# Down projection of a decoder trunk: three of each eight channel-block pairs by seven products of block sums

## The chip, the cores and the metric

The kernel runs on one core of a Trainium2 chip. The metric is the device time in microseconds (us) of one execution. The engines are named PE (TensorE, matmuls), DVE (VectorE), ACT (ScalarE), POOL (GpSimd) and SP (SyncE, which issues most DMAs); PEld is the weight load of TensorE, which overlaps its matmuls.

## The reference

Two decoder layers on 256 tokens with a model width of 2048, all in float32. Each layer has an attention part (two head groups) and an MLP with 8192 hidden channels:

```python
mixed = jnp.concatenate([o_gla, o_sb], axis=-1)
x = x + jnp.einsum('bse,ed->bsd', mixed, w_o)

hm = rms_norm(x, mlp_norm)
up = jnp.square(jax.nn.relu(jnp.einsum('bsd,df->bsf', hm, w_up)))
return x + jnp.einsum('bsf,fd->bsd', up, w_down)
```

The change concerns the last line: 256 tokens x 8192 channels times a 8192 x 2048 matrix, once in each of two layers, added to the residual.

## The kernel before

Every float32 factor is cut into an exact high and a low part of the type fp32r, and a product is three matmuls: high by high, high by low, low by high. For weights, ACT copies the loaded tile `raw` into the high part `whi` (L325), and DVE subtracts it for the low part `wlo` (L327), in pieces of 128 x 1024 numbers. `whi` and `wlo` have four buffers each and `raw` three, so the splits run ahead of the matmuls by up to four pieces (half-units).

The MLP goes through the 8192 hidden channels in four quarters of 2048. For a quarter, up projection (`mlp_up`) makes 16 blocks of 128 channels, with the channels on partitions: `unit_t` computes 256 columns (L391, L395), `join` adds the high and the low sums (ACT copy L405, DVE add L406), then come relu with the norm's row (L888), square (L892), and the split into high and low activations (L893, L894). Down projection (`mlp_down(q)`) then multiplies the quarter by its 2048 rows of `w_down`, in four units of 512 columns. A unit (`unit`) is 16 channel blocks x 2 token tiles x 3 matmuls of 128 x 512 (L344, L345, L346) into two PSUM banks, the tile `acc`; at its end DVE adds the unit to the residual `xb` (L919, 128 x 1024; at the program's end L910 with a store). PSUM holds two `acc` tiles of two banks each and four single banks `ps`, for the whole program.

The code's order is six groups of up (of four in a quarter, two units each), down of the first quarter, four groups of up, and so on. The framework has a scheduler that orders each engine's queue anew; the order on an engine is therefore not that of the code. Each engine works off its queue in order.

At a layer's end (`residual`) the residual blocks also go through transposes on PE (`norm_operand`, L261), which make the next layer's operand, and through sums of squares.

The functions that the change touches:

Of the kernel before, what the change touches and what calls it, by code (L numbers as in the profile page):

```python
# [39 lines left out]
def trunk_kernel(  # L40
# [19 lines left out]

    cpool = ctx.enter_context(tc.tile_pool(name="const", bufs=1))
# [5 lines left out]
    accp = ctx.enter_context(tc.tile_pool(name="acc", bufs=2, space=PSUM))  # L67
    psp = ctx.enter_context(tc.tile_pool(name="ps", bufs=4, space=PSUM))

    uid = [0]  # L70

    def nm(s):
        uid[0] += 1
        return f"{s}_{uid[0]}"
# [4 lines left out]
    def ps_tile():  # L79
        return psp.tile([P, 512], F32, tag="ps", name=nm("ps"))  # L80

    def acc_tile():
        return accp.tile([P, 2, 512], F32, tag="acc", name=nm("acc"))

    def tmp(tag, shape, dt=F32, bufs=2):
        return tpool.tile(list(shape), dt, tag=tag, name=nm(tag), bufs=bufs)
# [18 lines left out]
    kdz = cpool.tile([P, 3, 512], F32, name="kdz")  # L105

    def build_constants():
        nc.vector.tensor_copy(ident16, ident)

        # strictly causal mask of a diagonal block, keys on partitions: 0 where s < t  # L110
# [5 lines left out]
        # suffix sums: -1 where j >= s (j on partitions)  # L116
# [9 lines left out]
        # 1 where s <= c and both lie in one chunk (s on partitions)  # L126
# [8 lines left out]
        # scan multiplier: 0 at the start of each chunk  # L135
# [4 lines left out]
        # exp(last - cum) * k, tokens on partitions, one chunk's rows kept per entry  # L140
        nc.gpsimd.memset(kdz, 0.0)

# [82 lines left out]
    def inv_rms(ss, n, width):  # L225
        """(ss / width + EPS) ** -0.5, [P, n], with one Newton step."""
# [9 lines left out]
    class Operand:  # L236
        """Activations with channels on partitions: [P, 2 blocks, (high, low), T] tiles."""
# [15 lines left out]
    def norm_operand(op, n, key, l):  # L253
        """Residual block n -> operand blocks 4n.. (scaled by the gain)."""
# [316 lines left out]
    for l in range(DEPTH):  # L571
# [306 lines left out]
        # MLP  # L878
        up = {}

        def mlp_up(i):
            q, g = divmod(i, 4)
            if g == 0:
                up[q] = Operand()
# [83 lines left out]
```

## Time and profile before

| | |
|---|---|
| Time, median of 3 runs (lowest to highest) | 2248.5 us (2248.33 to 2249.91) |
| Profiled execution: span from first to last instruction | 2247.4 us |
| Its own time | some 1.1 us beside the span, if it ran as the median did |
| TensorE clock granted | 1.000 |
| PE busy | 2238.0 us, 11436 matmuls |
| DVE busy | 1315.8 us |
| ACT busy | 1085.9 us |
| Bytes moved, mean rate | 409.04 MB, 182 GB/s |

The runs lie within 1.6 us of each other. The page gives busy time as a share of the span, over all stages; which engine another waits for is in the view of the waits, and what a single stage does is in the windows and the timeline.

### The profile page before, as it was taken

To read this page: it belongs to the slowest core of one execution; us is meant where nothing else is said; L and a number is where in the kernel's file an instruction comes from. 1 tells how busy PE (TensorE), PEld (TensorE's weight loads), DVE (VectorE), ACT (ScalarE), POOL (GpSimd) and SP (SyncE) were. 2 spreads that over 40 slices of the span, in tenths; PEclk is the share of its full clock that TensorE was granted. 3 is DMA by queue.
4 is the path that set the end of the run, shared out by engine and by line. 5 is a ranking of instruction groups with operands and counts; after the bars stand their busy time and mean duration, and the time that the engine had idled before them with its cause. 6 is when DMAs were issued, how large, how long until landed. Compare 5 with 4: busy or idle time off the path is not lost.

```text
span 2247.4 us, 28019 instructions
## 1 busy us (share of the span) xinstructions
PE 2238.0 (100%) x11436; PEld 1883.2 (84%) x11436; DVE 1315.8 (59%) x1508; ACT 1085.9 (48%) x1363; POOL 37.7 (2%) x67
## 2 busy tenths in 40 slices
PE   9999999999999999999999999999999999999999
PEld 7988778888888888888888887888888888888887
DVE  5777565666556556555557765656655554565554
ACT  5555355555345445445445553555543453454442
POOL 0020000000000000000000200000000000000000
PEclk9999999999999999999999999999999999999999
DMA  6555445665565566565546544456665655655554
GB/s 226 190 157 163 150 143 195 187 188 188 200 191 186 190 188 187 190 196 192 180 149 202 169 152 149 164 184 182 191 194 191 187 188 191 192 186 197 189 197 141
DMA packets 283622, 409.04 MB, mean 182 GB/s; under 512 B 6651, under 2 KB 162883, under 8 KB 283493
## 3 DMA queue, kind: packets, MB, share of 16 engines
q1 hardware_dynamic: 283492, 407.24, 56.6%
q8 instruction: 90, 1.47, 0.3%
q14 instruction: 40, 0.32, 0.0%
HBM read 405.12 MB, written 2.10 MB: 181 GB/s over the span
## 4 chain that ended last, share of the span: by engine, by line
PE 98%; DVE 1%; issue 0%; DMA 0%; ACT 0%; POOL 0%; SPq 0%; DVEq 0%; POOLq 0%
PE acc L391 24%; PE acc L344 19%; PE acc L346 19%; PE acc L345 19%; PE acc L395 12%; PE ps L261 1%; PE ps L806 1%; PE ps L818 1%; PE ps L765 0%; PE ps L507 0%; PE ps L453 0%; PE ps L542 0%; PE ps L471 0%; DVE wlo L327 0%; DMA raw<-in_w_in_dram 0%
## 5 line engine op out<-in xcount | busy, mean ns | idle before, releaser
L327 DVE TENSOR_TENSOR wlo<-raw,whi 128x1024 fp32r<-128x1024 f32 (+2 forms) x786 | 944.4, 1204 | 805.2 <-ACT whi L325 804.6
L325 ACT ACTIVATE whi<-raw 128x1024 fp32r<-128x1024 f32 (+2 forms) x786 | 816.4, 1041 | 1036.7 <-PE acc L346 642.8
L391 PE MATMUL acc<-act,whi 128*128 128x512 f32 x2304 | 811.2, 397 | 0.0
L344 PE MATMUL acc<-whi,act 128*128 128x512 f32 (+2 forms) x1984 | 766.6, 386 | 1.4 <-ACT act L269 1.1
L345 PE MATMUL acc<-wlo,act 128*128 128x512 f32 (+2 forms) x1984 | 760.3, 383 | 0.4 <-DVE wlo L327 0.4
L346 PE MATMUL acc<-whi,act 128*128 128x512 f32 (+2 forms) x1984 | 759.9, 383 | 0.0
L395 PE MATMUL acc<-act,wlo 128*128 128x256 f32 x2304 | 644.1, 280 | 0.0
L391 PEld LDWEIGHTS acc<-act,whi 128*128 128x128 f32 x2304 | 432.7, 188 | 104.0
L344 PEld LDWEIGHTS acc<-whi,act 128*128 128x128 f32 x1984 | 372.9, 188 | 76.5 <-issue 4.1
L395 PEld LDWEIGHTS acc<-act,wlo 128*128 128x128 f32 x2304 | 434.4, 189 | 0.4
L346 PEld LDWEIGHTS acc<-whi,act 128*128 128x128 f32 x1984 | 372.7, 188 | 73.8 <-issue 0.7
L345 PEld LDWEIGHTS acc<-wlo,act 128*128 128x128 f32 x1984 | 372.9, 188 | 71.7 <-DVE wlo L327 1.2
L406 DVE TENSOR_TENSOR t<-acc,t 128x512 f32<-128x512 f32 x72 | 49.2, 683 | 0.0
L894 DVE TENSOR_TENSOR act<-t,act 128x512 fp32r<-128x512 f32 x64 | 44.3, 692 | 6.2 <-ACT act L893 6.2
L893 ACT ACTIVATE act<-t 128x512 fp32r<-128x512 f32 x64 | 40.5, 634 | 11.8 <-PE acc L346 10.0
L888 DVE SCALAR_TENSOR_TENSOR t<-t,row 128x512 f32<-128x512 f32 x64 | 44.3, 692 | 2.2
L405 ACT ACTIVATE t<-acc 128x512 f32<-128x512 f32 x72 | 41.6, 578 | 0.0
L892 ACT ACTIVATE t<-t 128x512 f32<-128x512 f32 x64 | 39.4, 615 | 0.0
L919 DVE TENSOR_TENSOR xb<-acc,xb 128x1024 f32<-128x1024 f32 x24 | 29.4, 1224 | 9.6 <-PE acc L346 9.6
L413 DVE TENSOR_REDUCE st<-t 128x4 f32<-128x512 f32 (+1 forms) x36 | 21.6, 622 | 0.5
L301 POOL COPY bc<-st 128x128 f32<-128x128 f32 x8 | 2.6, 320 | 1149.5 <-DVE st L233 1059.9
L412 DVE TENSOR_TENSOR t<-on 128x512 f32<-128x512 f32 x16 | 11.9, 743 | 16.1 <-ACT on L532 16.1
(137 smaller groups left out, 669.4 us busy)
## 6 DMA issues: line engine op xcount, KB each, us to landing
raw<-in_w_up_dram SPq DMA_DIRECT2D x128, 1024.0 KB, 5.8
raw<-in_w_down_dram SPq DMA_DIRECT2D x128, 1024.0 KB, 5.0
raw<-in_w_in_dram SPq DMA_DIRECT2D x84, 1024.0 KB, 5.2
raw<-in_w_o_dram SPq DMA_DIRECT2D x32, 1024.0 KB, 5.1
raw<-in_w_in_dram SPq DMA_DIRECT2D x14, 512.0 KB, 6.7
raw<-in_w_in_dram SPq DMA_DIRECT2D x8, 544.0 KB, 3.9
out_dram<-xb SPq DMA_DIRECT2D x8, 256.0 KB, 2.3
xb<-in_x_dram SPq DMA_DIRECT2D x3, 512.0 KB, 7.9
```

Of the source, the lines that this page charges most:

```text
L325: newest["hi"] = nc.scalar.activation(h, r, AF.Copy).ins
L327: newest["lo"] = nc.vector.tensor_tensor(lo[:, q : q + step, :width], r, f32(h), ALU.subtract).ins
L344: nc.tensor.matmul(o, xh[:, sl], whi[:, j, :width], start=first, stop=False)
L345: nc.tensor.matmul(o, xh[:, sl], wlo[:, j, :width], start=False, stop=False)
L346: st["mm"] = nc.tensor.matmul(o, xl[:, sl], whi[:, j, :width], start=False, stop=last).ins
L391: nc.tensor.matmul(acc[:, f, :], whi[:, j, sl], op.both(k), start=(k == 0), stop=False, skip_group_check=True,)
L395: nc.tensor.matmul(acc[:, f, T:], wlo[:, j, sl], xh, start=False, stop=(k == KT - 1), skip_group_check=True,)
L405: nc.scalar.activation(t, acc[:, :, T:], AF.Copy)
L406: nc.vector.tensor_tensor(t, acc[:, :, :T], t, ALU.add)
L888: nc.vector.scalar_tensor_tensor(t, t, 0.0, nxt["row"].unsqueeze(1).to_broadcast([P, 2, T]), ALU.max, ALU.mult,)
L893: nc.scalar.activation(d[:, :, 0, :], t, AF.Copy)
L894: nc.vector.tensor_tensor(d[:, :, 1, :], t, f32(d[:, :, 0, :]), ALU.subtract)
```

## The change

**Products.** A step of down projection is now one pair of channel blocks (256 channels) by 1024 columns, and a quarter is two halves of eight steps. Tokens, channels and columns are each two blocks, so a step is a 2 x 2 by 2 x 2 block product. For the pairs 1, 4 and 7 (`fast`), it is done by seven block products of sums and differences (Strassen's scheme in Winograd's form), 7 x 3 = 21 matmuls; the other pairs take eight products, 24 matmuls, arranged so that they add into four of the same sums.

**Banks.** The sums of a half stay in seven PSUM banks, `m1` to `m7`, over all eight steps, and are put together in `xb` at the half's end by eleven additions on DVE of 128 x 512 (`plain` and `shared`, L1020) and a copy on ACT (L1104). PSUM is divided anew for that: seven banks and one `ps` during down projection, as before in the rest.

**Weights.** In a fast step DVE forms sums of weight blocks from `raw`: `t13` (L1049, 128 x 1024), a sum in place over the second block (`b12`), and `t4` (L1020, 128 x 512 each). They are split as other weights are (L1002 high, L1005 low). For nine of the ten plain steps of a quarter, the low part of the second half is made otherwise: ACT writes the negative high part (`early`, L997), and a DMA from POOL's queue adds `raw` to it (L998, 512 KB). Raw tiles are 128 x 2 x 1024, three buffers and one more, `raw2`, for each fourth step; a step's load is issued three steps ahead.

**Activations.** After the square of an up unit, `up_forms` makes differences of its 128 x 128 blocks on DVE (L942 to L949): four operations for a fast pair, one for another; ACT and DVE split them too (L933, L934).

**Order.** All four groups of up of a quarter, then its down projection.

The core of the diff:

```diff
+        def up_forms(op, i, t):
+            a11, a21, a12, a22 = (t[:, k, r * P : (r + 1) * P] for k in range(2) for r in range(2))
+            e = tmp("t2", [P, 3, P], bufs=4)
+            if fast(i):
+                d = op.x[i] = tmp("sx", [P, 3, 2, P], F32R, bufs=3)
+                nc.vector.tensor_tensor(e[:, 2, :], a21, a11, ALU.subtract)
+                nc.vector.tensor_tensor(a21, a21, a22, ALU.subtract)
+                nc.vector.tensor_tensor(e[:, 0, :], a11, a21, ALU.subtract)
+                nc.vector.tensor_tensor(e[:, 1, :], a12, e[:, 0, :], ALU.subtract)
+            else:
+                d = op.x[i] = tmp("cx", [P, 2, 2, P], F32R, bufs=5)
+                e = e[:, :2, :]
+                nc.vector.tensor_tensor(e, t[:, :, :P], t[:, :, P:], ALU.subtract)
+            split(op.pair(i), t)
+            split(d, e)
+
+        def fast(i):
+            return i % 3 == 1
...
         def mlp_down(q):
-            for n in range(4):
-                ud = unit(up[q], w_down[l], q * KT * P, n * 512, 512, split=(end and n == 3))
...
+            def early(x):
+                if x in low2 or x >= len(steps) or x == 0 or fast(steps[x][1]):
+                    return
+                r = raws[x][:, :, 512:]
+                lo = low2[x] = act_tile(F32R, (P, 2, 512))
+                nc.scalar.activation(lo, r, AF.Copy, scale=-1.0)
+                nc.gpsimd.dma_start(f32(lo), r, accum_op=ALU.add)
...
+                if fast(j):
+                    t13 = tmp("ts", [P, 2, 512], bufs=2)
+                    t4 = tmp("t4", [P, 512], bufs=1)
+                    b12 = r[:, 0, 512:]
+                    ends = r.rearrange("p k (c n) -> p (k c) n", c=2)[:, ::3, :]
+                    nc.vector.tensor_tensor(
+                        t13, ends, b12.unsqueeze(1).to_broadcast([P, 2, 512]), ALU.add
+                    )
+                    w = parts(r[:, 1, :].rearrange("p (c n) -> p c n", c=2))
+                    mm(2, blk(1, 0), w, 0, final)
+                    mm(3, ext(1), w, 1, final)
+                    add(b12, t13[:, 0, :], r[:, 1, 512:])
+                    add(t4, b12, r[:, 1, :512])
+                    w = parts(t4.unsqueeze(1), 1)
+                    mm(4, blk(1, 1), w, 0, final)
+                    tick()
+                    w = parts(t13)
+                    mm(5, blk(0, 1), w, 0, final)
+                    mm(7, ext(2), w, 1, final_fast)
+                    w = parts(r[:, 0, :].rearrange("p (c n) -> p c n", c=2))
+                    mm(1, blk(0, 0), w, 0, final_fast)
+                    mm(6, ext(0), w, 1, final_fast)
+                    tick()
+                else:
+                    w = parts(r[:, :, :512])
+                    for k in range(2):
+                        mm(2, blk(k, 0), w, k, final and k == 1)
+                        mm(4, blk(k, 1), w, k, final and k == 1)
+                    tick()
+                    w = parts(r[:, :, 512:], lo=low2.get(x))
+                    for k in range(2):
+                        mm(5, blk(k, 1), w, k, final and k == 1)
+                    for k in range(2):
+                        mm(3, ext(k), w, k, final and k == 1)
+                    tick()
...
-        for i in range(6):
-            mlp_up(i)
-        for q in range(3):
+        for q in range(4):
+            if q:
+                att_psum()
+            for g in range(4):
+                mlp_up(q, g)
+            down_psum()
             mlp_down(q)
-            for i in range(6 + 4 * q, min(10 + 4 * q, 16)):
-                mlp_up(i)
-        mlp_down(3)
```

**Two places in the queues.** The first is ACT's queue where up projection gives way to down projection in layer 0's first quarter; the later quarters have the same rows. Before: `raw_819` and the raws after it are weights of later units, `acc_800` is the last up unit and `t2_811` its result on chip.

```order
L325 ACTIVATE whi_822_4770<-raw_819_4752 128x1024
L405 ACTIVATE t2_811_4709<-acc_800_4624 128x512
L325 ACTIVATE whi_825_4788<-raw_824_4786 128x1024
L892 ACTIVATE t2_811_4709<-t2_811_4709 128x512
L325 ACTIVATE whi_827_4804<-raw_824_4786 128x1024
L325 ACTIVATE whi_830_4822<-raw_829_4820 128x1024
```

After: `raw_792` holds the weights of step 1, the first fast one, `t4_803` and `ts_802` (t13) are sums of them; `raw_793` and `raw2_794` are the weights of steps 2 and 3; `t2_778` is the last up unit's result, `t2_779` its differences.

```order
L1002 ACTIVATE whi_804_4467<-raw_792_4418 128x1024
L1002 ACTIVATE whi_806_4479<-t4_803_4465 128x512
L437 ACTIVATE t2_778_4385<-acc_767_4300 128x512
L929 ACTIVATE t2_778_4385<-t2_778_4385 128x512
L1002 ACTIVATE whi_808_4486<-ts_802_4464 128x1024
L933 ACTIVATE act_781_4396<-t2_778_4385 128x2x256
L933 ACTIVATE sx_780_4391<-t2_779_4390 128x3x128
L997 ACTIVATE act_795_4424<-raw_793_4420 128x1024
L997 ACTIVATE act_801_4461<-raw2_794_4422 128x1024
L1002 ACTIVATE whi_810_4496<-raw_792_4418 128x1024
```

The last up unit's copy, square and split stood between high parts for later units. Now they stand, with two more 128 x 1024 copies (L997) and the split of the differences, ahead of the high part `whi_810` that step 1's last six matmuls read.

The second is DVE's queue where the down projection of layer 0's first quarter gives way to up projection (later quarters alike). Before, with the last drain of the quarter in the second row:

```order
L327 TENSOR_TENSOR wlo_905_5315<-raw_903_5312,whi_904_5314 128x1024
L919 TENSOR_TENSOR xb3_99<-acc_876_5131,xb3_99 128x1024
L327 TENSOR_TENSOR wlo_907_5335<-raw_903_5312,whi_906_5334 128x1024
L327 TENSOR_TENSOR wlo_913_5366<-raw_911_5363,whi_912_5365 128x1024
```

After, where `wlo_912` and `wlo_914` are low parts for the last fast step, and `wlo_921` and `wlo_923` those of up projection's first weights, `raw_919`:

```order
L1005 TENSOR_TENSOR wlo_912_5031<-ts_905_5007,whi_911_5029 128x1024
L1020 TENSOR_TENSOR xb2_100<-m2__854_4744,xb2_100 128x512
L1005 TENSOR_TENSOR wlo_914_5041<-raw2_887_4900,whi_913_5039 128x1024
L1020 TENSOR_TENSOR xb2_100<-m4__855_4745,xb2_100 128x512
L1020 TENSOR_TENSOR xb3_101<-m5__857_4747,xb3_101 128x512 x2
L1020 TENSOR_TENSOR xb3_101<-m3__856_4746,xb3_101 128x512
L1020 TENSOR_TENSOR xb2_100<-m1__858_4748,xb2_100 128x512
L359 TENSOR_TENSOR wlo_921_5074<-raw_919_5071,whi_920_5073 128x1024
L1020 TENSOR_TENSOR t2_915_5054<-m6__859_4749,t2_915_5054 128x512
L359 TENSOR_TENSOR wlo_923_5094<-raw_919_5071,whi_922_5093 128x1024
```

One drain of 128 x 1024 stood between low parts made well ahead. Now six drains of 128 x 512 stand between the last fast step's low parts and the first of up projection.

More of the change, by code (lines that the diff above doesn't have):

```diff
@@ L860, in residual @@
         def residual(op, n, key, ll, ssq, acc, done):
-            nc.vector.tensor_tensor(xb[n], acc, xb[n], ALU.add)
+            if acc is not None:
+                nc.vector.tensor_tensor(xb[n], acc, xb[n], ALU.add)
             after(1, lambda: norm_operand(op, n, key, ll))
@@ L902, in mlp_down @@
         def mlp_down(q):
[L903 to L912 removed]
+            op = up[q]
+            end = q == 3 and l + 1 == DEPTH
@@ new lines, in mlp_down, with mm, add @@
+            banks, begun = {}, set()
+            def mm(m, a, w, c, last):
+                (ah, al), (wh, wl) = a, w
+                o = banks[m]
+                nc.tensor.matmul(o, ah, wh[:, c], start=m not in begun, stop=False)
+                begun.add(m)
+                nc.tensor.matmul(o, ah, wl[:, c], start=False, stop=False)
+                nc.tensor.matmul(o, al, wh[:, c], start=False, stop=last)
+            def add(dst, a, b, sub=False):
+                nc.vector.tensor_tensor(dst, a, b, ALU.subtract if sub else ALU.add)
```

159 lines of the change are left out of this document (129 added, 30 removed).

## The prediction

> **What bounds the kernel now.** I read the page first: span, busy time of each engine, and the chain that ended last.
>
> ```profile
> span 2247.4 us, 28019 instructions
> PE 2238.0 (100%) x11436; PEld 1883.2 (84%) x11436; DVE 1315.8 (59%) x1508; ACT 1085.9 (48%) x1363; POOL 37.7 (2%) x67
> PE 98%; DVE 1%; issue 0%; DMA 0%; ACT 0%; POOL 0%; SPq 0%; DVEq 0%; POOLq 0%
> ```
>
> TensorE sets the end nearly alone: 98% of the chain is matmul following matmul. Next the waits by pair (total us, count, longest us).
>
> ```profile
> DVE wlo L327 <- ACT whi L325: 804.6, 641, 4.4
> ACT whi L325 <- PE acc L346: 642.8, 415, 3.9
> PE acc L344 <- ACT act L269: 1.1, 1, 1.1
> ```
>
> The splits wait for TensorE (ScalarE's high part for a buffer that matmuls free, VectorE's low part for the high one); TensorE's own longest such wait on ScalarE adds up to 1.1 us in the whole program. Then two units of a down projection by the window view (after the window: sum, then PE, PEld, DVE, ACT, POOL, granted clock, DMA share, GB/s), and a stretch of up projection.
>
> ```profile
> 574.00:595.75 21.75, 21.75 (x97) 18.02 (x96) 10.93 (x10) 8.48 (x9) 0.00 (x0) 1.00 0.56 193
> 595.75:617.51 21.76, 21.76 (x97) 18.02 (x96) 10.94 (x10) 8.49 (x9) 0.00 (x0) 1.00 0.59 194
> 541.00:552.20 11.20, 11.20 (x66) 9.81 (x66) 6.84 (x7) 5.97 (x8) 0.00 (x0) 1.00 0.57 194
> ```
>
> A unit is 96 matmuls in 21.76 us, so 0.2267 us each at clock 1.00, while VectorE works half of the time, ScalarE 39%, the DMA engines 0.56 to 0.59. So every matmul less is worth 0.2267 us, as long as three engines that have been half idle keep up with a pattern that asks for more of them.
>
> **What the change removes.** A quarter of a layer's down projection had 4 x 96 = 384 matmuls. Now each of its two halves (1024 columns) runs eight steps, one for each pair of channel blocks: five plain steps of 24 matmuls and three seven-product ("fast") steps of 21, so 183 instead of 192. Eight quarters x 18 = 144 matmuls; 144 x 0.2267 = **-32.6 us**. The matmuls keep their shape (128x512). (The Trainium skill, page "TensorE: Matmul & The Clock Gate", section "Back-to-back issue gap", states a sustained 131 ns for N=512; by that the gain would be an estimated 18.9 us. The trace's spacing is 227 ns, and it decides.)
>
> **What it adds.** Durations, by form (count | busy, mean ns):
>
> ```profile
> L327 DVE TENSOR_TENSOR wlo<-raw,whi 128x1024 fp32r<-128x1024 f32 x750 | 919.3, 1228 | 785.2 <-ACT whi L325 784.6
> L327 DVE TENSOR_TENSOR wlo<-raw,whi 128x512 fp32r<-128x512 f32 x20 | 13.6, 686 | 9.9 <-ACT whi L325 9.9
> L325 ACT ACTIVATE whi<-raw 128x1024 fp32r<-128x1024 f32 x750 | 793.6, 1060 | 1003.4 <-PE acc L346 615.7 <-PE acc L391 385.1 <-ACT t L278 1.8
> L406 DVE TENSOR_TENSOR t<-acc,t 128x512 f32<-128x512 f32 x72 | 49.2, 683 | 0.0
> L888 DVE SCALAR_TENSOR_TENSOR t<-t,row 128x512 f32<-128x512 f32 x64 | 44.3, 692 | 2.2
> L833 DVE TENSOR_TENSOR on<-on,act 128x256 f32<-128x256 f32 x16 | 5.7, 418 | 0.0
> L919 DVE TENSOR_TENSOR xb<-acc,xb 128x1024 f32<-128x1024 f32 x24 | 29.4, 1224 | 9.6 <-PE acc L346 9.6
> L893 ACT ACTIVATE act<-t 128x512 fp32r<-128x512 f32 x64 | 40.5, 634 | 11.8 <-PE acc L346 10.0
> L892 ACT ACTIVATE t<-t 128x512 f32<-128x512 f32 x64 | 39.4, 615 | 0.0
> raw<-in_w_down_dram SPq DMA_DIRECT2D x128, 1024.0 KB, 5.0
> out_dram<-xb SPq DMA_DIRECT2D x8, 256.0 KB, 2.3
> ```
>
> A fast step asks VectorE for three 1024-wide low parts (3 x 1.228), t13 (1.22, as L919), b12, t4 and t4's low part (3 x 0.69): 6.98 us against its 21 x 0.2267 = 4.76 us of TensorE. A plain step asks for one low part or two (the second half's goes to ScalarE and an accumulating DMA): 1.2 to 2.5 of 5.44. Per half that is about 3 x 6.98 + 5 x 1.3 + 7.6 of drains (eleven of 0.69) = 35 of 183 x 0.2267 = 41.5 us. On average it fits. With three fast steps apart and four split buffers, my schedule of a half's middle leaves some 0.9 us before TensorE would wait: no cost inside a half. Costs come at the **seams**, where up projection and down projection, or two halves, meet. The one shown is that of layer 0 between a quarter's up and its down, in before:
>
> ```profile
> 552.02 0.40 PE L344 MATMUL acc<-whi,act 128*128 128x512 f32 x1
> 552.10 1.06 ACT L325 ACTIVATE whi<-raw 128x1024 fp32r<-128x1024 f32 x1 [1.71 <-PE acc L391]
> 553.07 0.58 ACT L405 ACTIVATE t<-acc 128x512 f32<-128x512 f32 x1
> 554.95 1.06 ACT L325 ACTIVATE whi<-raw 128x1024 fp32r<-128x1024 f32 x1 [1.30 <-PE acc L346]
> 555.91 0.61 ACT L892 ACTIVATE t<-t 128x512 f32<-128x512 f32 x1
> 553.20 1.23 DVE L327 TENSOR_TENSOR wlo<-raw,whi 128x1024 fp32r<-128x1024 f32 x1 [1.55 <-ACT whi L325]
> 554.34 0.68 DVE L406 TENSOR_TENSOR t<-acc,t 128x512 f32<-128x512 f32 x1
> 555.06 0.69 DVE L888 SCALAR_TENSOR_TENSOR t<-t,row 128x512 f32<-128x512 f32 x1
> 573.99 1.22 DVE L919 TENSOR_TENSOR xb<-acc,xb 128x1024 f32<-128x1024 f32 x1 [0.40 <-PE acc L346]
> 575.13 1.22 DVE L327 TENSOR_TENSOR wlo<-raw,whi 128x1024 fp32r<-128x1024 f32 x1
> ```
>
> These rows give the steps between starts: ScalarE 0.97 after a 1024-wide op (552.10 to 553.07), VectorE 1.14 (573.99 to 575.13), 0.72 where an op needs the one before it (554.34 to 555.06); without that need I take 0.6. Up's leftovers (copy, join, relu, square, split) cost nothing today, because the split at 552.10 is for weights used three half-units later.
>
> *(a) Up to down, 8 times.* Time 0 is the first down matmul. The orders in the section on the change show ScalarE's queue. VectorE: t4's low part to 1.43, join 2.02, relu 2.75, then t13 for step 4, which stands ahead of the up unit's own differences and waits for its weights (buffer free at -1.65, load 5.0): 3.35 to 4.58; then two sums and the four small differences (0.28 each for 128 columns, a line through 418 ns at 256 and 692 at 512) to 6.67. ScalarE: high part 0.08 to 0.71, join's copy 1.19, square 3.4, t13's high part 4.37, split 6.22, then the differences' split, ready only at 6.67, to 7.2; two early copies of 0.97 to 9.13; only then the high part of step 1's last weights, to 10.1. TensorE wants it after 24 + 15 matmuls, at 8.84: 1.2 us; its low part is out at 11.36, wanted at 10.35: 1.0. **2.2 us each, 17.6.** In the first quarter of a layer the last up result lies in the banks of the first products, so that TensorE waits for the join, at 2.0, instead: the same price.
>
> *(b) Half to half.* The drains are five to eight operations of 0.69 for VectorE, but the next half's first step is plain and already split: between 0 and 1.9 (as in c); I take 0.5, nearer to 0 as only the later splits queue behind drains. Six times: 3. In layer 0's last quarter transposes and squares of the next norm run here through a single bank: 3. In layer 1's last, two fast steps follow each other (2 x 6.98 for VectorE in 2 x 4.76: 4.4 short), and loads queue behind the output stores on SP: 5.
>
> *(c) Down to up, 6 times.* VectorE's order (section on the change) puts the drains of m2, m4, m5, m5, m3, m1 ahead of the low part of up's first weights. From the start of the last fast step, m1 is complete at 4.25 and drained to 5.7, the low part comes at 6.85; TensorE wants it at 4.76 + 0.23 = 4.99: **1.9 each, 11.4.**
>
> *(d) Layer 0 to 1.* 1.9 again, and the transposes of xb2 and xb3, which wait for their last drains (12.6 and 13.3 against 9.4 by the same count): 3.5; 5.4.
>
> The accumulating DMAs (512 KB, nine per quarter, on POOL's queue) have no row in before: between the 2.3 us of a 256 KB store and two loads of 5.0 = 10; I take 4.6, twice the store, nearest in kind. Step 2's second half has from 8.1 to 15.4, 7.3 us, so it is hidden.
>
> Sum of costs: 17.6 + 3 + 3 + 5 + 11.4 + 5.4 = 45.4. From 2247.4 - 32.6 + 45.4 = 2260.2, and the profiled execution lies 1.1 us under the 2248.5 median: **2261**.
>
> Bounds: (a) 0 if the schedule hides it, to 3.4 with one more 1.2 us op ahead; (b) 0 to 1.9, 5 and 8; (c) 1.2 (one low part late) to 3.1; (d) 1.2 to 5.4. Low 8.4 gives 2224; high 27.2 + 11.4 + 5 + 8 + 18.6 + 5.4 = 75.6 gives 2292.
>
> **Rivals.** *The seams are covered (faster).* Point: ScalarE delivers the high part of step 1's last weights by 8.8 after the first down matmul. If t13 for step 4 does not hold up the small differences, so that the split at 6.67 starts by 5.4, (a) is gone, and (b) with it. Left: 6 x 1.2 + 1.2 + 3 = 11.4 to 12. 2247.4 - 32.6 + 12 + 1.1 = **2228**. For it: engines half idle, splits running ahead. Against it: the queues are in order, and VectorE's load at the seam is the largest. Chance 0.33.
>
> *Accumulates late (slower).* If they take 10 us, not 7.3, step 2's second half is 2.7 late at eight starts (21.6) and step 3's by 2.2 (17.6): **2300**. Today's DMA share of 0.58 becomes about 0.60 (same bytes in less time) plus 0.17 for 4.7 MB more per 83 us quarter counted once (3.1 us of all engines per MB, from 0.58 x 21.76 / 4.2 MB): 0.77. The Trainium skill, page "Collectives: The Full Stack", section "The bandwidth ceiling: the fold count and why AG ≠ RS ≠ AR", says that an add in the DMA needs two source reads; by that the share would be an estimated 0.94. No run here shows it yet. Chance 0.12.
>
> *VectorE binds in each fast step.* If nothing of 6.98 - 4.76 is absorbed: 48 x 2.2 = 107, **2323**. Against it: the plain steps between give 4 us each. Chance 0.05.
>
> **How the numbers follow.** Forecast 0.50, covered 0.33, late accumulates 0.12, bound 0.05. The range 2224 to 2300 holds the first three. Within 0.2% (what a measurement of this kernel can tell from no change) is 2244 to 2253: costs of 28 to 37, the lower end of the forecast's own range of 2240 to 2292; of its 0.50 I give 0.08 to that and 0.03 to faster. Faster 0.33 + 0.03 = 0.36, same 0.08, slower 0.39 + 0.12 + 0.05 = 0.56.
>
> **What would show it.** Right: TensorE's count 144 lower; its waits, now near nothing, total some 45 us, in groups of about 2 us at the eight starts of a down projection, released by ScalarE's high or VectorE's low parts, and at the six starts of up by VectorE's low part. Wrong: waits under 15 us in sum (covered); waits on an accumulating DMA or on weight loads; or waits at every fast step.

## The result, and the profile after

The changed kernel takes 2298.57 us (median of 4, 2296.98 to 2300.35), the kernel before 2248.63 us beside it: ratio 1.0221, 95% interval 1.0206 to 1.0235. It is slower by 50 us, where 12.5 were forecast.

The page: span, busy times, DMA queues, chain.

```profile
span 2295.6 us, 28960 instructions
PE 2239.8 (98%) x11292; PEld 1861.8 (81%) x11292; DVE 1548.2 (67%) x2016; ACT 1253.4 (55%) x1611; POOL 125.9 (5%) x140
q1 hardware_dynamic: 250724, 407.24, 54.3%
q0 software_dynamic: 19584, 37.75, 9.7%
PE 77%; DMA 9%; DVE 7%; issue 5%; ACT 1%; POOL 0%; SPq 0%; POOLq 0%; ACTq 0%
```

The 144 matmuls are gone (11436 to 11292). But the chain that ended last is no longer matmuls alone: 98% before, 77% now, with DMA, VectorE and waits between. The waits and the DMAs that answer to it (waiter, releaser: total us, times, longest; the DMAs: count, size, median us to landing):

```profile
ACT act L997 <- DMA raw<-in_w_down_dram: 106.4, 53, 4.2
DVE ts L1049 <- DMA raw<-in_w_down_dram: 13.5, 17, 4.0
raw<-in_w_down_dram SPq DMA_DIRECT2D x128, 1024.0 KB, 7.6
act<-raw POOLq DMA_DIRECT2D x72, 512.0 KB, 6.1
```

A load of down weights takes 7.6 us instead of 5.0, and ScalarE's early copies stand 106 us at the head of its queue for one. Windows of the second quarter of layer 0, down and then up (columns as in the prediction), and before them the same down quarter of the kernel before, which took 86.84 us for 384 matmuls:

```profile
729.51:816.35 86.84, 86.84 (x386) 71.91 (x384) 44.58 (x38) 35.48 (x35) 0.00 (x0) 1.00 0.58 191
```

```profile
691.03:781.01 89.98, 86.10 (x367) 67.95 (x366) 59.29 (x71) 53.50 (x58) 10.84 (x9) 1.00 0.80 227
781.25:871.77 90.52, 88.90 (x512) 78.05 (x511) 67.89 (x86) 48.18 (x61) 0.00 (x0) 1.00 0.64 198
```

Now 366 matmuls take 89.98 us. At 0.2267 each they would take 83.0: 7 us are lost in one quarter. Where, is in TensorE's timeline: its rows with an idle time in brackets, from four places (start of layer 0's first quarter; the first and the second fast step of the second quarter; the start of up projection behind the first quarter).

```profile
510.68 0.50 PE L1014 MATMUL m__784_4409<-whi,act 128*128 128x512 f32 x1 [1.93 <-DVE t L438]
700.82 0.50 PE L1014 MATMUL m__1044_5875<-whi,act 128*128 128x512 f32 x1 [0.62 <-ACT whi L1002]
702.08 0.50 PE L1016 MATMUL m__1044_5875<-wlo,act 128*128 128x512 f32 x1 [0.76 <-DVE wlo L1005]
720.04 0.50 PE L1016 MATMUL m__1044_5875<-wlo,act 128*128 128x512 f32 x1 [1.82 <-DVE wlo L1005]
602.40 0.38 PE L427 MATMUL acc<-act,wlo 128*128 128x256 f32 x1 [1.62 <-DVE wlo L359]
```

The first three and the last are the waits of the prediction's (a) and (c). The fourth, inside a half, it had at nothing. ScalarE's and VectorE's rows ahead of it:

```profile
710.33 1.06 ACT L997 ACTIVATE act<-raw 128x1024 fp32r<-128x1024 f32 x1 [2.98 <-DMA raw<-in_w_down_dram]
716.89 1.23 DVE L1049 TENSOR_TENSOR ts<-raw 128x1024 f32<-128x1024 f32 x1 [0.69 <-DMA raw<-in_w_down_dram]
718.15 0.69 DVE L1020 TENSOR_TENSOR raw<-ts,raw 128x512 f32<-128x512 f32 x1
718.76 2.35 DVE L1005 TENSOR_TENSOR wlo<-raw,whi 128x1024 fp32r<-128x1024 f32 x2
```

An early copy waits 2.98 us for its load at the head of ScalarE's queue. Then t13 of the next fast step (716.89) waits 0.69 us for its own at the head of VectorE's, and it and the sum behind it stand ahead of the low part (718.76) that TensorE wants.

And there is a loss that is no wait. Windows of 3.41 us around such waits (the number ahead of the DMA share is the granted clock):

```profile
508.23:511.64 3.41, 1.48 (x8) 1.03 (x7) 1.99 (x3) 1.36 (x3) 0.00 (x0) 1.00 0.69 268
699.39:702.80 3.41, 2.03 (x8) 1.14 (x7) 2.18 (x3) 3.41 (x5) 2.21 (x2) 1.00 0.61 104
880.29:883.70 3.41, 1.90 (x8) 1.00 (x7) 2.18 (x3) 3.41 (x5) 2.33 (x2) 1.00 0.57 97
883.70:887.11 3.41, 3.41 (x10) 2.63 (x9) 1.69 (x2) 1.98 (x2) 0.00 (x0) 0.50 1.06 178
716.44:719.85 3.41, 1.78 (x8) 1.13 (x6) 2.92 (x3) 2.57 (x3) 0.00 (x0) 1.00 1.12 205
719.85:723.26 3.41, 3.22 (x14) 2.69 (x15) 3.00 (x4) 1.06 (x1) 0.00 (x0) 1.00 0.78 189
1061.21:1064.62 3.41, 1.82 (x8) 0.94 (x7) 2.18 (x3) 3.41 (x5) 2.10 (x2) 1.00 0.64 109
1064.62:1068.03 3.41, 3.41 (x10) 2.65 (x9) 1.47 (x2) 1.75 (x2) 0.00 (x0) 0.50 1.07 186
```

Behind the stretches in which TensorE was busy for 1.90 and 1.82 us the clock is 0.50 for the next 3.41 us, in which matmuls start 0.43 us apart: 1.7 us lost. Behind 2.03 us it stays 1.00, but so it does behind the 1.78 us ahead of 719.85, so the busy time of this view does not decide alone. Eight stretches at half clock lie in the changed kernel, seven of them in down projection; the one before has none until its end.

All 80.8 us of cost (2295.6 less 2247.4 - 32.6), from the starts of successive matmuls less 0.2267 us each: inside down projection 67.4, of which 30.2 are waits for high or low parts, 7.5 matmuls that follow slowly behind a wait, 10.9 half clock, 10.5 spacing that is a little wider all through (0.2303), 8.2 other waits. Outside: 4.4 at the two first quarters' starts, 4.2 in the first up projections (wider spacing), 1.2 at the starts of up, some 4 between the layers.

### The profile page after: what moved, and what is told of

Read it like the earlier page. It is cut to its first block, busy times and chain, and to the rows that moved or that the text cites. A ratio compares the mean times of both kernels' runs of the same rounds, so it can differ in the third digit from the quotient of the medians.

```text
span 2295.6 us, 28960 instructions
## 1 busy us (share of the span) xinstructions
PE 2239.8 (98%) x11292; PEld 1861.8 (81%) x11292; DVE 1548.2 (67%) x2016; ACT 1253.4 (55%) x1611; POOL 125.9 (5%) x140
## 3 DMA queue, kind: packets, MB, share of 16 engines
q0 software_dynamic: 19584, 37.75, 9.7%
## 4 chain that ended last, share of the span: by engine, by line
PE 77%; DMA 9%; DVE 7%; issue 5%; ACT 1%; POOL 0%; SPq 0%; POOLq 0%; ACTq 0%
PE acc L423 21%; PE acc L427 11%; PE acc L376 9%; PE acc L377 9%; PE acc L378 9%; DMA raw<-in_w_down_dram 6%; DVE wlo L1005 3%; DMA act<-raw 2%; DVE xb L1020 1%; DVE wlo L359 1%; ACT whi L1002 1%; DVE ts L1049 1%; PE ps L293 1%; PE ps L841 1%; PE ps L853 1%
## 5 line engine op out<-in xcount | busy, mean ns | idle before, releaser
L359 DVE TENSOR_TENSOR wlo<-raw,whi 128x1024 fp32r<-128x1024 f32 (+2 forms) x530 | 630.3, 1193 | 389.9 <-ACT whi L357 389.4
L357 ACT ACTIVATE whi<-raw 128x1024 fp32r<-128x1024 f32 (+2 forms) x530 | 544.0, 1031 | 585.1 <-PE acc L423 314.0
L427 PEld LDWEIGHTS acc<-act,wlo 128*128 128x128 f32 x2304 | 435.0, 189 | 12.5 <-DVE wlo L359 12.3
L376 PE MATMUL acc<-whi,act 128*128 128x512 f32 (+2 forms) x960 | 368.4, 384 | 0.5 <-ACT whi L357 0.5
L377 PE MATMUL acc<-wlo,act 128*128 128x512 f32 (+2 forms) x960 | 362.2, 377 | 2.0 <-DVE wlo L359 2.0
L378 PE MATMUL acc<-whi,act 128*128 128x512 f32 (+2 forms) x960 | 361.6, 377 | 0.0
L1002 ACT ACTIVATE whi<-raw 128x1024 fp32r<-128x1024 f32 x256 | 262.6, 1054 | 122.9 <-PE acc L423 18.1
L1005 DVE TENSOR_TENSOR wlo<-raw,whi 128x1024 fp32r<-128x1024 f32 x184 | 221.6, 1220 | 106.6 <-ACT whi L1002 106.1
L376 PEld LDWEIGHTS acc<-whi,act 128*128 128x128 f32 x960 | 180.9, 188 | 35.6 <-issue 4.1
L377 PEld LDWEIGHTS acc<-wlo,act 128*128 128x128 f32 x960 | 180.9, 188 | 33.9 <-DVE wlo L359 3.0
L378 PEld LDWEIGHTS acc<-whi,act 128*128 128x128 f32 x960 | 180.7, 188 | 33.8 <-issue 0.7
L998 POOL DMA_DIRECT2D act<-raw x72 | 86.8, 1236 | 1314.6 <-ACT act L997 1213.5
L997 ACT ACTIVATE act<-raw 128x1024 fp32r<-128x1024 f32 x72 | 75.2, 1057 | 106.4 <-DMA raw<-in_w_down_dram 106.4
L1005 DVE TENSOR_TENSOR wlo<-ts,whi 128x1024 fp32r<-128x1024 f32 x48 | 58.7, 1223 | 64.8 <-ACT whi L1002 64.8
L1049 DVE TENSOR_TENSOR ts<-raw 128x1024 f32<-128x1024 f32 x48 | 58.6, 1221 | 13.6 <-DMA raw<-in_w_down_dram 13.5
L1005 DVE TENSOR_TENSOR wlo<-t,whi 128x512 fp32r<-128x512 f32 x48 | 33.1, 689 | 51.4 <-ACT whi L1002 51.4
L1002 ACT ACTIVATE whi<-ts 128x1024 fp32r<-128x1024 f32 x48 | 50.5, 1052 | 30.9 <-PE m__1623_9131 L1017 4.5
```

The source lines that it names most:

```text
L357: newest["hi"] = nc.scalar.activation(h, r, AF.Copy).ins
L359: newest["lo"] = nc.vector.tensor_tensor(lo[:, q : q + step, :width], r, f32(h), ALU.subtract).ins
L376: nc.tensor.matmul(o, xh[:, sl], whi[:, j, :width], start=first, stop=False)
L377: nc.tensor.matmul(o, xh[:, sl], wlo[:, j, :width], start=False, stop=False)
L378: st["mm"] = nc.tensor.matmul(o, xl[:, sl], whi[:, j, :width], start=False, stop=last).ins
L427: nc.tensor.matmul(acc[:, f, T:], wlo[:, j, sl], xh, start=False, stop=(k == KT - 1), skip_group_check=True,)
```

## The experiments

Each ran once, with the kernel before timed beside it, unless a median is given. That kernel gave 2248 to 2255 us at different times, so some 5 us between variants say nothing unless they were timed together. By their first letters these were a to d, e to h, i to l; then `m_dma_only`, `n_after_pad`, `o_frame_plain` and `q_mid`; then `o_frame_plain2` and `q_mid2`. Theories: **queue** (fast steps ask more of VectorE and ScalarE than their in-order queues deliver in time), **DMA** (accumulates hold raw tiles and slow loads), **matmul** (spacing and clock of TensorE itself).

**Early copies and accumulating DMAs.** `c_no_accum` drops both, for the low parts on VectorE.

```diff
             def early(x):
-                if x in low2 or x >= len(steps) or x == 0 or fast(steps[x][1]):
-                    return
+                return
```

> No early copies and no accumulating DMAs: all low parts on VectorE. That takes 72 x 1.06 us off ScalarE and adds 72 x 1.22 = 88 us to VectorE. DMA theory: the loads of w_down fall from 7.6 to about 5 us, the sums of weights (t13) no longer wait for them at the head of VectorE's queue, and the waits at the last low part of pair 4 go: 2275 to 2285. Queue theory: VectorE has some 40.5 us of work in a half of 41.5, its waits grow: 2300 to 2330.

2270.98 us, 27.6 less than the change: DMA theory's side, though VectorE has more to do (1627 us busy against 1548). Loads take 5.9 us; t13 still waits for them (45.5 us). The two halves of the mechanism:

```diff
# l_copy_only
-                nc.gpsimd.dma_start(f32(lo), r, accum_op=ALU.add)
# m_dma_only
-                nc.scalar.activation(lo, r, AF.Copy, scale=-1.0)
-                nc.gpsimd.dma_start(f32(lo), r, accum_op=ALU.add)
+                nc.gpsimd.dma_start(f32(lo), r)
# both
-                    w = parts(r[:, :, 512:], lo=low2.get(x))
+                    w = parts(r[:, :, 512:], lo=None)
```

> The change, with the early negative copies on ScalarE still made (their result unused) but without the accumulating DMAs; the low parts come from VectorE as in c_no_accum (2271.0 us). It splits the 27.6 us between the two halves of that mechanism. If early copies that wait at the head of ScalarE's queue for their weights are the cost (106 us of such waits in the change), the time stays near the change's: 2288 to 2298. If the DMAs are (holding raw tiles, slowing loads to 7.6 us), it falls to c_no_accum's: 2271 to 2277.

> The counterpart of l_copy_only (2280.0 us): the nine DMAs per quarter of 512 KB from raw to an activation tile are still made on POOL's queue, as plain copies that add nothing and whose result is unused; the early copies on ScalarE are not, and the low parts come from VectorE. Between c_no_accum (2271.0, neither) and the change (2298.6, both). If the DMAs hold raw tiles and slow the loads of w_down, the time is some 18 us over c_no_accum, 2285 to 2292, with loads at 7 us or more. If it was the copies and their waits alone, 2271 to 2275.

2279.98 and 2293.91 us against the 2270.98 of `c_no_accum`: the copies alone cost 9, the DMAs alone 23 (three runs timed apart, so each within some 5 us), both 27.6, so they overlap. The DMAs are the larger part, but not as expected in `m_dma_only`, by slow loads. Its waits and DMAs:

```profile
DVE ts L1048 <- DMA raw<-in_w_down_dram: 70.6, 30, 5.5
raw<-in_w_down_dram SPq DMA_DIRECT2D x128, 1024.0 KB, 5.8
act<-raw POOLq DMA_DIRECT2D x72, 512.0 KB, 7.1
q0 software_dynamic: 10368, 37.75, 4.3%
```

Loads take 5.8 us as without the DMAs, yet t13 waits for them 70.6 us instead of 45.5: they come late. A raw tile is free for the next load only when the DMA that reads it has landed; that this delays the load is inferred, as the DMA's own competition was not tried apart. And `m_dma_only` copies without adding: the same 37.75 MB take 4.3% of the DMA engines' span (row `q0`), in the change 9.7%, and there the loads took 7.6 us. The 23 us are thus what plain copies cost; what the adding costs on top was not tried alone.

**The start of a down projection.** `b_low_2_3_dve` takes out the two early copies that the prediction's (a) named, and with them their accumulating DMAs (16 of 72).

```diff
-                if x in low2 or x >= len(steps) or x == 0 or fast(steps[x][1]):
+                if x in low2 or x >= len(steps) or x in (0, 2, 3) or fast(steps[x][1]):
```

> Steps 2 and 3 of the first half make their low part on VectorE instead of by early copy and accumulating DMA, so that two 128x1024 copies (2 x 0.97 us) no longer stand ahead of the high part of step 1's last weights. Queue theory: that high part comes at about 8.2 us after the first down matmul instead of 10.1, ahead of need; the waits at the 39th and 40th matmul (0.8 to 1.0 and 1.03 us) shrink to 0.3 at most in six quarters, and the half-clock stretches that follow them in three quarters go: 6 x 1.6 + 3 x 1.7 = 15 us less, 2284. DMA theory (lateness comes from loads and accumulates in flight): no more than the share of two accumulates in nine, some 2 to 4 us less, 2295. If VectorE is the bound there, the wait moves to later low parts: 2298 or more.

2282.75 us, 15.8 less, as queue theory had it: waits for ScalarE's high parts in down projection fall from 7.6 to 2.3 us, the half clock from 10.9 to 4.5, other waits a little. As copies and DMAs went together here, `l_copy_only`, which keeps the copies and drops every DMA, tells them apart. ScalarE's queue in the change, then TensorE's rows in `l_copy_only` at the same matmuls of the same quarter:

```profile
697.83 1.99 ACT L997 ACTIVATE act<-raw 128x1024 fp32r<-128x1024 f32 x2
699.73 2.93 ACT L1002 ACTIVATE whi<-raw 128x1024 fp32r<-128x1024 f32 x3
```

```profile
699.93 0.50 PE L1013 MATMUL m__1053_5884<-whi,act 128*128 128x512 f32 x1 [0.84 <-ACT whi L1001]
701.19 0.75 PE L1015 MATMUL m__1053_5884<-wlo,act 128*128 128x512 f32 x1 [0.76 <-DVE wlo L1004]
```

The pair of waits stays in all six quarters that had it: the copies ahead of the high part cause it, not the DMAs.

**No fast steps in the change's frame.**

```diff
         def fast(i):
-            return i % 3 == 1
+            return False
```

(with eight `cx` tiles, four banks, and the nine accumulates as they were)

> No pair by seven products: all eight pairs by 24 matmuls, with the change's tiles, four of its PSUM banks, its order and the same nine accumulating DMAs in a quarter, so 144 matmuls more than with the change. If the fast steps cause the loss (VectorE's and ScalarE's queues), the waits inside down projection go and only the start of a layer's first quarter (2 x 2.2 us) and half-clock stretches there stay: 2250 to 2260, faster than the change by 40 or more. If the frame causes it (block layout, PSUM divided anew, DMAs, order of up and down), the 32.6 us of matmuls come on top of it: 2310 to 2330.

2294.07 us: between the two. Without any seven products the frame costs 44 us over the kernel before beside it (2250.0); the fast steps add 37 and save 32.6. Here ScalarE's early copies wait 174.8 us for loads.

**Spacing of matmuls.** `a_ext_from_act` lets the matmuls on differences read activation blocks.

```diff
-                    return e[:, i, 0, :], e[:, i, 1, :]
+                    return blk(i % 2, 0)
```

> All work is done and all differences are still made, but the matmuls that read the tiles of differences (cx, sx) as their stationary operand read the activation blocks instead, so the sums are of other numbers. After the change, matmuls with cx or sx start 231 to 237 ns apart, with the activations 227 to 229. If the place or the tile of the stationary operand sets that, the mean spacing in down projection falls from 0.2303 to about 0.227 us: 8 x 341 x 0.0033 = 9 to 10 us less, 2288. If it is something else (a busier memory, the phase in which matmuls and weight loads run), the spacing and the time stay: 2298.

Both sides hold in part: spacing's excess in down projection falls from 10.5 to 2.9 us, but the time is 2304.88: the waits for split parts in down projection rise from 30.2 to 37.5 us, and four of the six up projections that follow take 92.3 us instead of 90.5. Where TensorE waits for others, faster matmuls only wait longer. Whether alignment is behind the spacing, `k_pad` tells (below), and `n_after_pad` does the same in the change:

```diff
+    pad = spool.tile([P, 32], F32, tag="pad", name="pad", bufs=1)
+    nc.vector.memset(pad, 0.0)
     att_psum()
```

> The change with the one edit of k_pad: the MLP's pool 128 bytes higher. In k_pad the excess of spacing went to nothing and the time fell by 8.4 us, where TensorE hardly waits. In the change TensorE waits for split weights in every half, so that a faster matmul meets the same queue a little earlier: as in a_ext_from_act spacing falls by 8 us or more and waits rise by most of it: 2292 to 2299. If spacing adds to the end directly, 2288.

2298.05 us: nothing gained, though not in the way expected. Spacing's excess falls to 3.0 us, and down projection loses 61.0 instead of 67.4 us; but again four of the six up projections behind it take 92.3 us instead of 90.5. Taking the wider spacing away gains nothing in the change; why up projection slows is open.

**Order in VectorE's queue.**

```diff
-                    nc.vector.tensor_tensor(
-                        t13, ends, b12.unsqueeze(1).to_broadcast([P, 2, 512]), ALU.add
-                    )
+                    with tc.issue_after(newlo[0]) if newlo[0] else nullcontext():
+                        nc.vector.tensor_tensor(
+                            t13, ends, b12.unsqueeze(1).to_broadcast([P, 2, 512]), ALU.add
+                        )
```

(`newlo[0]` is the low part that VectorE was given last.)

> The change as it is, accumulating DMAs included, with the one edit of g_246_order: t13 behind the last low part of the step before. In the change t13 of step 7 stands ahead of step 4's last low part, for which TensorE waits 1.3 to 2.0 us in six of eight quarters, and similar waits of 0.2 to 0.8 follow in second halves: some 15 us in all. Head-of-queue theory: these go, 2298.6 - 15 = 2284. DMA theory (the weights or the low parts themselves are late): the waits move to t13's own step, 2295 to 2300.

2297.13 us. The wait at the second fast step (720.04 above) is gone in all quarters, but a new one stands in the second half of six quarters, all but each layer's last. In the second quarter, with VectorE's rows ahead of it:

```profile
744.67 0.79 PE L1015 MATMUL m__1111_6207<-whi,act 128*128 128x512 f32 x1 [2.12 <-ACT whi L1002]
737.92 1.22 DVE L1051 TENSOR_TENSOR ts<-raw 128x1024 f32<-128x1024 f32 x1
742.59 0.69 DVE L1021 TENSOR_TENSOR xb<-t,xb 128x512 f32<-128x512 f32 x1
743.19 0.68 DVE L1021 TENSOR_TENSOR t<-raw 128x512 f32<-128x512 f32 x1
```

So t13 at the head of the queue did hold the low part up. In the new place t13 itself (737.92) no longer waits for its load (1.2 us in all), but the sum `t4` that follows from it comes only at 743.19, behind the drains of the half before, and TensorE waits for its high part. The time is the one that DMA theory gave, and the wait did move to t13's own step, but there it is for other work in VectorE's queue, not for a late load.

**Banks.** From here on without accumulates.

```diff
-                    for m in (2, 4, 3, 5, 1, 6, 7):
+                    for m in (1, 6, 3, 5, 2, 4, 7):
```

> As c_no_accum (2271.0 us), and the seven banks are handed out in another order, so that the first products of a down projection (m2, m4) lie in banks 4 and 5, which up projection's accumulators do not use. If TensorE's 2.2 us at the start of each layer's first quarter is the wait for the last up unit's join in the same bank, both go, and the half-clock stretch that follows in layer 1 too (1.7): 2271 - 4.4 - 1.7 = 2265. If it waits there for something else (weights, the operand), 2271 stays.

2273.82 us, no gain. The wait for the join is gone (the first down matmul follows the last of up by 0.11 us, not 2.2), but a new one came, 2.45 us at each of six starts of up:

```profile
596.55 0.50 PE L423 MATMUL acc<-act,whi 128*128 128x512 f32 x1 [2.45 <-DVE t L1019]
```

The releaser is the drain of m6, which now lies where up's first accumulator goes: the bank conflict was moved from one seam to the other.

**Place of the fast pairs**, and the order of t13 again.

```diff
         def fast(i):
-            return i % 3 == 1
+            return i in (2, 4, 6)
...
-                for j in ((1, 0, 4, 2, 7, 3, 5, 6) if end and n2 else range(8))
+                for j in ((0, 2, 1, 4, 3, 6, 5, 7) if end and n2 else range(8))
```

> As e_banks, and the pairs by seven products are 2, 4 and 6 instead of 1, 4 and 7 (at the program's end 2, 4, 6 with a plain step before, between and behind). Queue theory: the first fast step of a half has one plain step more in front, the last has one behind it, so that the last low part of each half's first fast step (0.7 and 1.1 to 1.5 us in twelve halves of c_no_accum) and the stall between the last two halves (some 5 us) go; the fast steps, each with one plain step between, still need 6.98 + 2.45 of VectorE in 10.2 us: 2265 - 12 - 5 = 2248. If VectorE can't hold that density, waits of 0.5 to 1 us at each fast step: 48 x 0.5 = 24 us on 2248, 2270.

> As f_246, and the sum t13 of a fast step is queued on VectorE behind the last low part of the step before, so that a t13 that waits for its weights (45.5 us in 23 waits in c_no_accum) no longer stands ahead of low parts that are ready. If that head of the queue is what makes low parts late, another 5 to 8 us less than f_246; if the load itself is late for its own step, the same or slower by some us.

2249.09 us: 25 less than `e_banks` by the place of three steps (and the last half's order); waits for low parts in down projection fall from 16.4 to 0.5 us. A density of one fast step in two, which rival and bound had feared, is not the trouble; a fast step right behind a seam or right before one is. `g_246_order`: 2248.87, the same; some waits less, one half-clock stretch more.

**Drains.** `i_shared_first` drains m1, m6, m7 first; `j_banks2` uses the order (1, 6, 7, 3, 2, 4, 5); `k_pad` adds the pad.

```diff
-                if end:
-                    shared()
-                    plain()
-                else:
-                    plain()
-                    shared()
+                shared()
+                plain()
```

> As g_246_order (2248.9 us), and at the end of every half the shared sums (m1, m6, m7, complete since the last fast step) are drained ahead of the plain ones. In f_246 and g_246_order the first matmul of up projection follows 1.8 us after the last of down projection, six times, against 0.23 in the change: with e_banks' order m1 and m6 lie in the banks that up projection's first accumulator takes. If it waits for their drains, six gaps of 1.55 us go: 2248.9 - 9.3 = 2240. If it waits for the weights' low part behind the drains, whichever comes first, the gap stays: 2249.

> As i_shared_first, and the banks in the order m1, m6, m7, m3, m2, m4, m5, so that only m3 shares a bank with the last up unit of the later quarters, and m3 comes last in the first step. The waits for that unit's join at the 12th matmul (0.3 to 0.6 us in six quarters) go: 2 to 3 us less than i_shared_first.

> As j_banks2, and all tiles of the MLP's own pool lie 128 bytes higher, so that the tiles of differences (cx, sx) begin at the same place within 256 bytes as activations and weights do (192 instead of 64). a_ext_from_act showed that matmuls which read cx or sx as stationary operand are spaced some 8 ns wider. If alignment within 256 bytes does that, the excess of spacing in down projection (10.5 to 11.5 us over 0.2267 us each) falls to some 3 and the time by 7 to 8 us. If it is the region of memory or the phase between matmul and weight load, nothing changes.

2242.59, 2240.05 and 2231.61 us. The first is not timed together with `g_246_order`, but in its trace the gap before up projection falls from 1.78 to 0.23 us at all six starts, as expected. With the pad, spacing's excess goes from 11.4 to 1.4 us. TensorE's rows with `cx` as stationary operand, in the change and in `k_pad`:

```profile
707.46 0.40 PE L1014 MATMUL m__1042_5873<-whi,cx 128*128 128x512 f32 x1
707.70 0.40 PE L1016 MATMUL m__1042_5873<-act,cx 128*128 128x512 f32 x1
```

```profile
529.20 0.39 PE L1016 MATMUL m__787_4414<-whi,cx 128*128 128x512 f32 x1
529.43 0.39 PE L1018 MATMUL m__787_4414<-wlo,cx 128*128 128x512 f32 x1
529.65 0.39 PE L1019 MATMUL m__787_4414<-whi,cx 128*128 128x512 f32 x1
```

From 0.24 to 0.225: the tiles lie 128 bytes higher, and nothing else differs between `j_banks2` and `k_pad`.

**What the removed matmuls are worth.** `k_pad` without fast steps:

> k_pad (2231.6 us) with all eight pairs by 24 matmuls and four banks: 144 matmuls more, no sums of weights, no shared sums. If the seven products are worth their matmuls once nothing waits for their operands, 2231.6 + 32.6 less the 6 to 8 us of waits for drains at a half's start, which the plain sums do not cause: 2256 to 2260, slower than the kernel before by 6 to 10. If the frame alone brings the gain, 2240 or less.

> o_frame_plain (2290.1 us) with k_pad's list of seven banks, three of them unused, so that up projection's first accumulator takes banks that no sum was in. In o_frame_plain those banks held m3 and m5, drained last: TensorE waited 2.0 us at each of six starts of up projection, with half-clock stretches behind most of them. If that is its excess, 2290 less 6 x 3.5 and some 10 us of half-clock stretches in down projection: 2257 to 2260, which puts the worth of the 144 matmuls, against k_pad's 2231.6 us, at 25 to 29 us. If the frame itself is slow with plain steps, 2275 or more.

The first, 2290.07 us, missed, for a reason of its own: its list of banks (3, 5, 2, 4) put the sums drained last where up begins (1.58 us idle there on `DVE xb`, six times), and the first products of a down projection where the last up unit lies. The second cost more: at six starts of down projection TensorE waits for that unit's join, with half clock behind five of them.

```profile
689.67 0.53 PE L1016 MATMUL m__998_5766<-whi,act 128*128 128x512 f32 x1 [2.89 <-DVE t L440]
```

The second version, with `k_pad`'s list, has neither wait and gives 2253.31: 21.7 us above `k_pad` (not timed together), and 4.5 above the kernel before beside it. The block layout by itself thus costs little; most of the 44 us that `d_all_plain` lost is left to its early copies, DMAs and banks, and to the pad that it lacks.

**The version that the runs point to.** `k_pad` still waits 8 us for drains at the starts of second halves.

```diff
-                shared()
-                plain()
+                if n2:        # q_mid2: if n2 or end:
+                    shared()
+                    plain()
+                else:
+                    plain()
+                    shared()
```

> As k_pad (2231.6 us), but only a quarter's second half drains the shared sums first; the first half drains the plain ones first, so that m2 and m4, which the next half needs at once, come free earlier. k_pad waits 8 us in all for drains at the starts of second halves; g_246_order, with the plain sums first, next to nothing there. 5 to 7 us less than k_pad: 2225 to 2227, or 22 to 24 us below the kernel before. If the half after waits for the shared sums' drains instead, as late as before, 2231.

> As q_mid (2225.1 us), except that in the program's last quarter both halves drain the shared sums ahead of the plain ones, as the change does, since a block is stored right after its plain sums (q_mid stored the first half's blocks there before the shared sums were added to them). One start of a second half may wait up to 1 us more for m2's and m4's drains: 2225 to 2226.5, 1.1 to 1.2% below the kernel before.

`q_mid` 2225.10 (median of 4), but it leaves out the shared sums from the blocks that it stores first in the last quarter; `q_mid2`, which does all the work, 2223.61 us (2222.90 to 2224.43), against 2248.77 before: ratio 0.9887, interval 0.9871 to 0.9904. Its page and, in a quarter of down projection, its window:

```profile
span 2222.4 us, 28573 instructions
PE 2213.3 (100%) x11292; PEld 1858.8 (84%) x11292; DVE 1634.8 (74%) x2089; ACT 1181.9 (53%) x1539; POOL 39.1 (2%) x68
PE 97%; DVE 2%; issue 0%; ACT 0%; DMA 0%; POOL 0%; SPq 0%; POOLq 0%; ACTq 0%; DVEq 0%
684.00:769.00 85.00, 85.00 (x381) 70.52 (x380) 77.22 (x88) 45.82 (x51) 0.00 (x0) 1.00 0.57 194
```

VectorE is busy 91% of that window, more than in the change (59.29 of 89.98), and TensorE never waits there. It is 29.7 us below `o_frame_plain2`: with the waits gone, the 144 matmuls are worth nearly their 32.6.

## Why the prediction was wrong

- **The gain, 32.6**: right in count; it stood, and was overlaid.
- **(a) 2.2 at each start**: right in place, cause and size: 0.7 to 1.0 for the high part, 1.03 for the low, in six quarters; 2.2 for the join in the two first. `b_low_2_3_dve` and `l_copy_only` together show the copies as the cause, and `e_banks` the bank. The half clock that followed some of these waits was in no term.
- **(b)**: 0.5 for the ordinary halves was above what came (0.1 to 0.2 just at the seam); the two last quarters were under-sized: their downs lost 14.0 and 13.8 us, 7 more than the others, for 3 and 5.
- **(c) 1.9 at each start of up**: the wait is there, 1.62, but cost only 0.2, since the up phase that follows it took 90.53 us with the wait and 90.33 in the kernel before without: its matmuls ran closer together. The term was 1.2, not 11.4; why they close up is not settled. The wait does not fix the pace: in `f_246`, behind the same gap of 1.78 us, two of six up phases took 88.7 us and four 90.4.
- **(d) 5.4 between the layers**: some 4, of which 1.7 were half clock.
- **"No cost inside a half"** is the step that failed. The waits at the second fast step and in second halves add up to some 16 us. The term stood at 0: its 0.9 us of room was reckoned with loads of 5.0 us, which took 7.6. So t13 waits for its load at the head of VectorE's queue, and early copies at the head of ScalarE's, in the middle of a half as at the seam, where the prediction had seen it; `h_t13_order` shows t13's part at the second fast step.
- **"So it is hidden"**, of the accumulating DMAs, failed too. They took 6.1 us, near the 4.6 and short of the 7.3 allowed, and TensorE waited for one only once (1.8 us). Their cost lay elsewhere: with the early copies 27.6 us, by late loads and by copies at the head of ScalarE's queue. The rival of late accumulates gave the right time, 2300, by the wrong path; that was luck.
- **The DMA share**: 0.80 in the window above, near the 0.77 by a single count, but by chance. The adding queue (`q0`) took 9.7% of the span for 37.75 MB, 5.9 us of all engines per MB; the queue of the loads 3.1 (`q1`), the plain copies of `m_dma_only` 2.6. For one quarter that is 27.8 us, 0.31 of the window, not 0.17; the loads there took the other 0.49, not 0.60. The Trainium skill's page "Collectives: The Full Stack", section "The bandwidth ceiling: the fold count and why AG ≠ RS ≠ AR", states two source reads for the add of a ReduceScatter, by which the share would be the estimated 0.94. The trace agrees with the double count for the adding DMAs, though not with a share of 0.94; as their packets were also half as large (19584 against 10368), the reason for the factor is not shown.
- **Not in the sum at all**: the clock (10.9 us in down projection, 1.7 between the layers) and spacing (10.5 and 4.2). Taking spacing away brought nothing as long as TensorE waited; the clock is a cost that waits close together add.

What stays open: how the cost of the DMAs divides between held raw tiles, competition and the adding; what else decides the clock; and the spacing in up projection, closer behind (c) and wider in `a_ext_from_act` and `n_after_pad`.

## What to carry to other kernels

When TensorE is the bound and work is moved to engines that were half idle, what counts is not their busy time but what stands ahead in their queues at each seam: an instruction that waits for a DMA holds up everything behind it. Place the costly steps away from the seams and give the first products of a phase banks that the phase before freed early; that was worth more than the matmuls saved. When a bank or an order is changed to remove a wait, look at once at the other end of the same bank or queue.

## What the hardware showed

The granted clock fell to 0.50 for 3.41 us at a time. In the 3.41 us ahead, TensorE had been busy 1.90 us or less: 1.90 and 1.82 with two waits of 0.75 to 0.85 us, 1.48 with a single wait of 1.93. No threshold can be read from the busy time, as other stretches of the same grid, with 1.78 us (716.44, a single wait of 1.82 that reaches into the next stretch) or 2.03, were followed by full clock. The starts of the slow stretches (511.6, 883.7, 1064.6 us) lie whole multiples of 3.413 us apart (109 and 53). The Trainium skill, page "TensorE: Matmul & The Clock Gate", section "What's actually happening", states a free-running window of 3413 ns, which agrees; its section "HAM oscillation — how this bites in real kernels" gives the rule that idle gaps over some 3.4 us are to be avoided, and here gaps of under 1 us sufficed when two of them met in one window.

Matmuls whose stationary operand began 64 bytes past a multiple of 256 in its partition, the moving one 192, were spaced some 231 to 237 ns; with both at 192 (`k_pad`), 227. One pad of 128 bytes took 8.4 us off a kernel whose TensorE hardly waits (some 8 us for drains), and nothing off the change, where it does. Only these two placements were tried.
